# A layer's recurrence: the first two chunks' block products, exponentials and square roots put together

## Chip, cores and metric

The kernel runs on one core of a Trainium2 chip. The time is that of the device for one execution, in microseconds (us); of the kernel before it is 901.03, the median of three runs.

## What is computed

One layer over 512 positions of width 1024, in float32. After an RMS norm, one projection feeds three token mixers and their gates; then come the branches' projections, an output projection and a gated feed-forward part. The change is in the second mixer, a gated linear recurrence:

```python
r = jax.nn.sigmoid(jnp.einsum('bshi,hij->bshj', xb, w_rg).reshape(B, S, LRU_WIDTH) + b_rg)
i = jax.nn.sigmoid(jnp.einsum('bshi,hij->bshj', xb, w_ig).reshape(B, S, LRU_WIDTH) + b_ig)
log_a = (-LRU_C * r.astype(jnp.float32)) * jax.nn.softplus(-lru_lambda.astype(jnp.float32))
a = jnp.exp(log_a)
mult = jnp.sqrt(-jnp.expm1(2.0 * log_a))
b = mult * (i * xc).astype(jnp.float32)
# h[t] = a[t] * h[t-1] + b[t]
```

`xc` is a convolution of width 4 of the projection, and `w_rg` and `w_ig` are block-diagonal, 16 blocks of 64 x 64.

## The kernel before

Everything lies with channels on the 128 partitions and the 512 positions along the free axis. Each float32 product is made of three products of rounded parts: an operand is split on ACT into a high part (`whi`, L110) and on DVE into the rest (`wlo`, L111), and `mm3` (L278 to L280) multiplies high by high, high by low and low by high.

The stage of the change computes, on PE and in this order, four chunks of the recurrence's projection (`ps_lru`, two blocks of 128 channels each, so 256 of 1024) and four chunks of a branch's gate logits (`ps_gate_1`), as lru 0, 1, 2, gate 0, lru 3, gate 1, 2, 3. A chunk is 48 matmuls in two halves of 24, each half with a weight tile of its own; the halves are numbered, so that `whi14` and `whi15` are those of gate 0, 16 and 17 those of lru 3, 18 and 19 those of gate 1. Three weight tiles (`wp`, `bufs=3`) go round: the split of number n waits until PE has used number n - 3. Then the q, k and v projections (`ps_q`) begin, with weight halves 24, 25, 26 and so on.

The work of the recurrence on the other engines is cut into steps and laid in between. `lru_chunk(c)` (L596 on) emits the 48 matmuls of chunk c and gives back four functions:

- `conv` (L609): the convolution on DVE, out of PSUM;
- `split` (L615, L616): `xch` and `xcl`, the two parts of `xc`, on DVE;
- `both`: `gates(0)` and `gates(1)`, the products with the blocks (`lg`, L626: two PSUM tiles, each of three pairs of instructions of 64 rows, and the two of a pair run side by side), and on ACT eight sigmoids of 64 x 512 (`lr` L630, `li` L631);
- `tanh` (L635 on DVE, L638 on ACT).

Further steps are `lru_exp` (exponentials L655, square roots L661 on ACT), `lru_decay` (L666, L668 on DVE), `lru_input` (L674, L675 on DVE), `lru_scan` (L681 on DVE) and `lru_store` (L687 on ACT, L688 on DVE, two DMAs on POOL's queue). ACT holds one set of function tables at a time; sigmoid and tanh are in one set here, the exponential and the square root in two others, and where the next function is in another set an `ACT_TABLE_LOAD` stands ahead of it.

A list `bg` holds the steps. `step(...)` appends one entry, which may hold several functions, and `tick()` runs entries; an lru or gate chunk ticks four times, once behind each 12 matmuls. What a chunk's ticks run are thus the entries that were listed before it. `gate1(c)` (L717) emits a gate chunk and, behind it, `gate_store` (L570: two sigmoids of the PSUM tile into `gt1c`, and a store). The code's order is only the start: each engine's rows are arranged by a scheduler with priorities (weight splits get 60 and 200, `conv`, `split` and the first product of the convolution 300). Each engine then runs its rows strictly in the order in which they stand.

PSUM in this stage is a pool `pb` of four buffers of two banks each, named here by their first bank: 0, 2, 4, 6. A chunk takes one buffer; so does each of the two `lg` tiles of a chunk. A tile can only be written when the last reader of the one before it in its buffer is done. The recurrence's SBUF tiles come from 13 buffers of 4 KB a partition in the same manner.

Of the kernel before, what the change touches and what calls it, by code (L numbers as in the profile page):

```python
# [66 lines left out]
def layer_kernel(ctx: ExitStack, tc: tile.TileContext, x, xt, vecs, w_in, w_qkv7, w_gate7, w_pool, w_rg, w_ig,  # L67
# [340 lines left out]
    with ExitStack() as first:  # L408
# [308 lines left out]
        def gate1(c):  # L717
            gate_store(1, c, chan_chunk(("gate", 1, c), hn, 1, pb), True)
# [3 lines left out]
        def step(*fs):  # L722
            bg.append(lambda: [f() for f in fs])

        def of(f, c):
            return lambda: f(c)

        c0, s0, g0, t0 = lru_chunk(0)
        step(c0), step(s0), step(), step()
        c1, s1, g1, t1 = lru_chunk(1)  # L730
        step(c1), step(s1), step(g0), step(t0)
        c2, s2, g2, t2 = lru_chunk(2)
        step(of(lru_exp, (0,))), step(c2), step(s2), step(g1)
        gate1(0)
        step(of(lru_decay, 0), t1), step(of(lru_exp, (1,))), step(g2), step(of(lru_input, 0))
        c3, s3, g3, t3 = lru_chunk(3)
        step(c3), step(s3), step(of(lru_decay, 1), of(lru_scan, 0)), step(t2, of(lru_input, 1))
        gate1(1)
        step(of(lru_scan, 1)), step(g3, of(lru_store, 0)), step(t3, of(lru_store, 1)), step(of(lru_exp, (2, 3)))
        gate1(2)  # L740
        for f, c in ((lru_decay, 2), (lru_decay, 3), (lru_input, 2)):
            step(of(f, c))
# [927 lines left out]
```

## Time and profile before

| | |
|---|---|
| median of three runs (lowest, highest) | 901.03 us (900.64, 901.3) |
| the profiled execution | 900.73 us |
| its span, from the first instruction to the last | 899.0 us |
| PE busy | 893.4 us, 99% |
| DVE busy | 732.3 us, 81% |
| ACT busy | 523.2 us, 58% |
| POOL busy | 86.3 us, 10% |
| granted PE clock | full in every slice |

The page counts a matmul as busy from its start to its modelled end, 0.39 us, while they start 0.227 us apart; small waits of PE are hidden in that, and are read from the starts. In rows of the timeline the first number is the start from the beginning of the span, the second the duration; what stands in brackets is the idle time ahead and what ended it. A few per cent of the matmul records can be missing.

### The profile page before, as it was taken

Reading aid. Unit: us, or ns where it says so; the run is one execution under the profiler, and the core shown is the slowest. Engines: PE = TensorE matmul, PEld = TensorE weight load, DVE = VectorE, ACT = ScalarE, POOL = GpSimd, SP = SyncE. Lnnn points to the kernel's source line nnn. Section 1 sums busy time; section 2 is a strip of 40 time slices with the busy share of each in tenths; the row PEclk is TensorE's granted clock in tenths of the full one; section 3 lists DMA queues with packets and bytes.
Section 4 is the critical chain, followed back from the end, with each engine's and each line's share of the span. In section 5 each row is a group of like instructions: output and inputs, shape, how many; then the busy total and the mean of one; then the engine's idle time right before and its main releaser. Section 6 shows DMA issues by size and latency. Waiting matters only on the chain.

```text
span 899.0 us, 14052 instructions
## 1 busy us (share of the span) xinstructions
PE 893.4 (99%) x5491; PEld 794.2 (88%) x5491; DVE 732.3 (81%) x922; ACT 523.2 (58%) x722; POOL 86.3 (10%) x126
## 2 busy tenths in 40 slices
PE   9999999999999999999999999999999999999998
PEld 6888778788899888888888988889999999989998
DVE  7897897988786599967887696699888888799764
ACT  7554989556856556555664544454555555664532
POOL 1110002232332101000001100000000000101200
PEclk9999999999999999999999999999999999999999
DMA  9585347789682785734736865245543333866842
GB/s 337 147 303 156 115 127 215 234 286 242 181 260 71 233 235 190 220 118 141 223 91 152 184 177 170 94 131 152 141 117 95 111 102 125 225 167 122 180 99 94
DMA packets 116579, 151.98 MB, mean 169 GB/s; under 512 B 8096, under 2 KB 90016, under 8 KB 116512
## 3 DMA queue, kind: packets, MB, share of 16 engines
q1 hardware_dynamic: 104416, 107.30, 37.7%
q0 software_dynamic: 11952, 43.52, 20.6%
q8 instruction: 43, 0.70, 0.3%
q10 hardware_dynamic: 144, 0.26, 0.1%
q14 instruction: 24, 0.20, 0.1%
HBM read 130.61 MB, written 18.87 MB: 166 GB/s over the span
## 4 chain that ended last, share of the span: by engine, by line
PE 95%; DVE 2%; ACT 2%; issue 1%; DMA 0%; SPq 0%; DVEq 0%; ACTq 0%
PE ps_y L287 11%; PE ps_x L287 8%; PE ps_q L798 7%; PE ps_dy L287 5%; PE ps_dx L287 4%; PE ps_br L278 3%; PE ps_br L279 3%; PE ps_br L280 3%; PE ps_gate L701 2%; PE ps_bY L1238 2%; PE ps_gy L287 2%; PE ps_gate L280 2%; PE ps_bX L1238 2%; PE ps_gx L287 2%; PE ps_gate L279 2%; PE ps_gate L278 2%
## 5 line engine op out<-in xcount | busy, mean ns | idle before, releaser
L110 ACT ACTIVATE whi<-raw 128x1024 fp32r<-128x1024 f32 x73 | 77.2, 1058 | 85.3 <-PE ps_out L279 17.0
L111 DVE TENSOR_TENSOR wlo<-raw,whi 128x1024 fp32r<-128x1024 f32 x73 | 89.1, 1220 | 32.9 <-ACT whi L110 32.9
L111 DVE TENSOR_TENSOR wlo<-qw,whi 128x1024 fp32r<-128x1024 f32 x48 | 58.6, 1222 | 20.8 <-ACT whi L110 20.5
L110 ACT ACTIVATE whi<-qw 128x1024 fp32r<-128x1024 f32 x48 | 50.8, 1057 | 33.1 <-PE ps_q L798 18.6
L1403 ACT ACTIVATE wh_S<-w_S 128x1024 fp32r<-128x1024 f32 x36 | 38.2, 1064 | 35.5 <-PE ps_y L287 22.4
L1404 DVE TENSOR_TENSOR wl_S<-w_S,wh_S 128x1024 fp32r<-128x1024 f32 x36 | 43.8, 1220 | 6.2 <-ACT wh_S L1403 6.2
L1403 ACT ACTIVATE wh<-w 128x1024 fp32r<-128x1024 f32 x27 | 28.8, 1066 | 30.3 <-issue 11.9
L1494 POOL DMA_DIRECT2D dw<-in_w_down_dram x16 | 13.5, 846 | 325.9 <-DVE wl L1404 248.2
L1404 DVE TENSOR_TENSOR wl<-w,wh 128x1024 fp32r<-128x1024 f32 x27 | 32.9, 1220 | 10.0 <-ACT wh L1403 10.0
L1403 ACT ACTIVATE whdS<-dw 128x1024 fp32r<-128x1024 f32 x16 | 17.0, 1064 | 24.4 <-PE ps_dy L287 13.2
L1404 DVE TENSOR_TENSOR wldS<-dw,whdS 128x1024 fp32r<-128x1024 f32 x16 | 19.6, 1224 | 12.9 <-ACT whdS L1403 12.9
L1054 DVE TENSOR_TENSOR_SCAN E<-K,ahead 128x512 f32<-128x512 f32 (+3 forms) x32 | 25.3, 812 | 4.4 <-ACT K L1050 4.4
L278 PE MATMUL ps_br<-yHH,whi 128*128 128x512 f32 x64 | 25.3, 395 | 0.0
L278 PE MATMUL ps_lru<-HH,whi 128*128 128x512 f32 x64 | 25.2, 394 | 0.0
L278 PE MATMUL ps_br<-yph,whi 128*128 128x512 f32 x64 | 25.2, 394 | 0.0
L278 PE MATMUL ps_pool<-HH,whi 128*128 128x512 f32 x64 | 25.2, 393 | 0.0
L279 PE MATMUL ps_br<-ypl,whi 128*128 128x512 f32 x64 | 25.0, 391 | 0.0
L280 PE MATMUL ps_gate<-HH,wlo 128*128 128x512 f32 x64 | 25.0, 391 | 0.0
L278 PE MATMUL ps_gate<-HH,whi 128*128 128x512 f32 x64 | 25.0, 391 | 0.0
L280 PE MATMUL ps_br<-yph,wlo 128*128 128x512 f32 x64 | 25.0, 391 | 0.0
L279 PE MATMUL ps_br<-yHL,whi 128*128 128x512 f32 x64 | 25.0, 390 | 0.0
L279 PE MATMUL ps_pool<-HL,whi 128*128 128x512 f32 x64 | 25.0, 390 | 0.0
(717 smaller groups left out, 3426.3 us busy)
## 6 DMA issues: line engine op xcount, KB each, us to landing
raw<-in_w_in_dram SPq DMA_DIRECT2D x31, 512.0 KB, 5.2
qw<-in_w_qkv_dram SPq DMA_DIRECT2D x24, 512.0 KB, 6.8
w<-in_w_ffn_gate_dram SPq DMA_DIRECT2D x36, 256.0 KB, 4.1
w<-in_w_ffn_up_dram SPq DMA_DIRECT2D x36, 256.0 KB, 4.6
raw<-in_w_branch_dram SPq DMA_DIRECT2D x16, 512.0 KB, 4.4
dw<-in_w_down_dram POOLq DMA_DIRECT2D x16, 512.0 KB, 6.3
qw<-in_w_qkv_dram POOLq DMA_DIRECT2D x12, 512.0 KB, 7.6
qd<-r POOLq DMA_DIRECT2D x12, 512.0 KB, 7.2
```

Source lines behind the costliest of these rows:

```text
L110: act(hi, raw, AF.Copy)
L111: dve.tensor_tensor(lo, raw, hi.bitcast(F32), ALU.subtract)
L278: nc.tensor.matmul(ps, lh, rh, start=start, stop=False, skip_group_check=skip)
L279: nc.tensor.matmul(ps, lh, rl, start=False, stop=False, skip_group_check=skip)
L280: nc.tensor.matmul(ps, ll, rh, start=False, stop=stop, skip_group_check=skip)
L287: nc.tensor.matmul(o, a_[a][:, w, k, :], b_[b][:, k, :], start=first and n == k == 0, stop=last and n == 2 and k == 3, skip_group_check=True)
L701: nc.tensor.matmul(pss[n // 2][n % 2], w[:, k % 2, n * P:(n + 1) * P], hu[k][x_], start=k == 0 and w is wh and x_ == 0, stop=k == KT - 1 a ...
L798: nc.tensor.matmul(ps[:, a, :], b_[:, k, ts_], a_[:, kk, :], start=first and n == k == 0, stop=n == 2 and k == 3, skip_group_check=True)
L1054: dve.tensor_tensor_scan(E[:, c0:c0 + n][:, ::-1], K[:, c0 + 1:c0 + n + 1][:, ::-1], ahead[:, S - n:][:, ::-1], 0.0, ALU.mult, ALU.add)
L1238: nc.tensor.matmul(o, ah[x_][:, w, k, :], b[k][y_], start=first_ and n == k == 0, stop=n == 2 and k == 3, skip_group_check=True)
L1403: act(h, src, AF.Copy)
L1404: dve.tensor_tensor(l, src, h.bitcast(F32), ALU.subtract)
```

## The change

Only the list of steps is written in another order. The block products of chunks 0 and 1 (`g0`, `g1`) become one entry, run in gate 0's ticks and not in those of lru 2 and gate 0; their tanh (`t0`, `t1`) and then their exponentials and square roots (`lru_exp` of (0, 1), in place of one call for each) follow, and the steps behind them move by what that takes.

```diff
         c1, s1, g1, t1 = lru_chunk(1)
-        step(c1), step(s1), step(g0), step(t0)
+        step(c1), step(s1), step(), step()
         c2, s2, g2, t2 = lru_chunk(2)
-        step(of(lru_exp, (0,))), step(c2), step(s2), step(g1)
+        step(c2), step(g0, g1), step(s2, t0, t1), step(of(lru_exp, (0, 1)))
         gate1(0)
-        step(of(lru_decay, 0), t1), step(of(lru_exp, (1,))), step(g2), step(of(lru_input, 0))
+        step(of(lru_decay, 0)), step(of(lru_input, 0)), step(g2), step(of(lru_decay, 1), of(lru_scan, 0))
         c3, s3, g3, t3 = lru_chunk(3)
-        step(c3), step(s3), step(of(lru_decay, 1), of(lru_scan, 0)), step(t2, of(lru_input, 1))
+        step(c3), step(s3, of(lru_input, 1)), step(t2), step(of(lru_scan, 1))
         gate1(1)
-        step(of(lru_scan, 1)), step(g3, of(lru_store, 0)), step(t3, of(lru_store, 1)), step(of(lru_exp, (2, 3)))
+        step(of(lru_store, 0)), step(g3, of(lru_store, 1)), step(t3), step(of(lru_exp, (2, 3)))
         gate1(2)
```

**PE, around gate 0.** In the rows, `lg10` is chunk 1's first tile of block products and `lg11` its second; HH0 and HL0 are the two parts of the input's first half, HH1 and HL1 those of the second. Before, at the end of gate 0 (chunk 0's products are already done, in the middle of lru 2):

```order
L280 MATMUL ps_gate_1_0_809<-HH1_105,wlo15_753 128x512
L626 MATMUL lg10_886<-xch1_744,lwh_525 128x512 x2
L626 MATMUL lg10_886<-xcl1_745,lwh_525 128x512 x2
L626 MATMUL lg10_886<-xch1_744,lwl_526 128x512 x2
L626 MATMUL lg11_897<-xch1_744,lwh_525 128x512 x2
L626 MATMUL lg11_897<-xcl1_745,lwh_525 128x512 x2
L626 MATMUL lg11_897<-xch1_744,lwl_526 128x512 x2
L278 MATMUL ps_lru_3_912<-HH0_104,whi16_812 128x512
```

In the change, in the middle of gate 0 (behind the three rows of `lg00`, chunk 0's first tile, of which the last is shown):

```order
L626 MATMUL lg00_820<-xch0_668,lwl_526 128x512 x2
L626 MATMUL lg01_831<-xch0_668,lwh_525 128x512 x2
L626 MATMUL lg01_831<-xcl0_669,lwh_525 128x512 x2
L626 MATMUL lg01_831<-xch0_668,lwl_526 128x512 x2
L626 MATMUL lg10_842<-xch1_744,lwh_525 128x512 x2
L626 MATMUL lg10_842<-xcl1_745,lwh_525 128x512 x2
L626 MATMUL lg10_842<-xch1_744,lwl_526 128x512 x2
L626 MATMUL lg11_853<-xch1_744,lwh_525 128x512 x2
L626 MATMUL lg11_853<-xcl1_745,lwh_525 128x512 x2
L626 MATMUL lg11_853<-xch1_744,lwl_526 128x512 x2
L278 MATMUL ps_gate_1_0_783<-HH1_105,whi15_752 128x512
```

Four tiles of products now stand together, while gate 0's own tile is half done.

**ACT, behind the sigmoids of chunk 1.** `gt10` is gate 0's output, the last reader of its PSUM tile; `lt`, `lr` and `ls` are the tanh, the exponential and the square root, with the chunk's number. Before:

```order
L631 ACTIVATE li1_749<-lg11_897,bigx_206 64x512
L570 ACTIVATE gt10_908<-ps_gate_1_0_809,vt_69 128x512 x2
L110 ACTIVATE whi19_955<-raw19_953 128x1024
L638 ACTIVATE lt1_933<-lr1_748,cpos_112 128x512 x2
L655 ACT_TABLE_LOAD
L655 ACTIVATE lr1_748<-lr1_748,cneg_113 128x512 x2
L661 ACT_TABLE_LOAD
L661 ACTIVATE ls1_951<-lt1_933 128x1024
L630 ACT_TABLE_LOAD
L630 ACTIVATE lr2_872<-lg20_971,vt_69 64x512
```

In the change:

```order
L638 ACTIVATE lt1_892<-lr1_748,cpos_112 128x512 x2
L655 ACT_TABLE_LOAD
L655 ACTIVATE lr0_672<-lr0_672,cneg_113 128x512 x2
L110 ACTIVATE whi19_957<-raw19_955 128x1024
L655 ACTIVATE lr1_748<-lr1_748,cneg_113 128x512 x2
L661 ACT_TABLE_LOAD
L661 ACTIVATE ls0_912<-lt0_888 128x1024
L661 ACTIVATE ls1_914<-lt1_892 128x1024
L570 ACT_TABLE_LOAD
L570 ACTIVATE gt10_916<-ps_gate_1_0_783,vt_69 128x512 x2
L110 ACTIVATE whi20_1017<-raw20_1015 128x1024
L630 ACTIVATE lr2_886<-lg20_973,vt_69 64x512
```

`gt10`, which stood ahead of chunk 1's tanh, now stands behind the tanh, exponentials and square roots of both chunks. Ahead of the piece shown stand sixteen sigmoids (L630, L631) and chunk 0's tanh, with the split `whi18` between; the table loads from the first exponential to chunk 3's are six where they were nine.

**DVE, during gates 1 and 2.** `xch3` and `xcl3` are chunk 3's split, `wlo22` is gate 3's first weight. Before:

```order
L615 CAST xch3_1047<-xc3_1007 128x1024
L111 TENSOR_TENSOR wlo21_1056<-raw21_1053,whi21_1055 128x1024
L616 TENSOR_TENSOR xcl3_1048<-xc3_1007,xch3_1047 128x1024
L111 TENSOR_TENSOR wlo22_1101<-raw22_1098,whi22_1100 128x1024
L635 TENSOR_TENSOR li2_873<-li2_873,xc2_806 128x1024
L675 TENSOR_TENSOR ls1_951<-ls1_951,li1_749 128x1024
L681 SCALAR_TENSOR_TENSOR li1_749<-lt1_933,ls1_951 128x512 x2
```

In the change:

```order
L616 TENSOR_TENSOR xcl3_1052<-xc3_1011,xch3_1051 128x1024
L668 TENSOR_SCALAR lt1_892<-lt1_892 128x1024
L111 TENSOR_TENSOR wlo22_1103<-raw22_1100,whi22_1102 128x1024
L681 SCALAR_TENSOR_TENSOR li0_673<-lt0_888,ls0_912 128x512 x2
L674 SCALAR_TENSOR_TENSOR ls1_914<-lr1_748,ls1_914 128x1024
L635 TENSOR_TENSOR li2_887<-li2_887,xc2_780 128x1024
L675 TENSOR_TENSOR ls1_914<-ls1_914,li1_749 128x1024
L111 TENSOR_TENSOR wlo23_1165<-raw23_1162,whi23_1164 128x1024
L681 SCALAR_TENSOR_TENSOR li1_749<-lt1_892,ls1_914 128x512 x2
```

Chunk 0's scans (the rows of L681 that write `li0`) now stand behind `wlo22`. The tanh of chunk 2 on ACT takes the SBUF buffer of `lt0`, so it waits for these scans; before, it took another one. On ACT the split `whi22` stands ahead of that tanh, and behind it `gt11`, `whi23`, the copy `yh0` (L687) and chunk 3's sigmoids; before, `yh0` stood behind chunk 3's sigmoids.

**PSUM.** The rows name tiles, not buffers. Which buffer a tile gets goes by which is free first, and the built programs give:

| tile | before: buffer, tile ahead of it in there | change: buffer, tile ahead of it in there |
|---|---|---|
| ps_lru_0, ps_lru_1, ps_lru_2 | 6, 4, 2 | 6, 4, 2 |
| lg00, lg01 | 0; 6, lru_0 | 6, lru_0; 4, lru_1 |
| ps_gate_1_0 | 4, lru_1 | 0 |
| lg10, lg11 | 0, lg00; 6, lg01 | 2, lru_2; 6, lg00 |
| ps_lru_3 | 2, lru_2 | 4, lg01 |
| ps_gate_1_1 | 4, gate_1_0 | 0, gate_1_0 |
| ps_gx1, ps_gy1 (the last tiles of this pool) | 0; 4 | 2; 0 |
| ps_pool_1_0 (the first of the next stage) | bank 0, behind gx1 | bank 0, behind gy1 |

gx1 and gy1 are the last products of the third branch's gates; DVE reads them at L847, and the pool mixer's projection `ps_pool` follows on PE.

## The prediction

> **What bounds the kernel now.** I read the busy times first, then the view of waits for TensorE (PE) alone, then stretches of the part that the change touches, with the busy time of PE, PEld, DVE, ACT and POOL in that order.
>
> ```profile
> PE 893.4 (99%) x5491; PEld 794.2 (88%) x5491; DVE 732.3 (81%) x922; ACT 523.2 (58%) x722; POOL 86.3 (10%) x126
> ...
> PE warm_ps L422 <- DVE warm L301: 1.5, 1, 1.5
> PE ps_gate L701 <- ACT hu L437: 0.5, 1, 0.5
> PE ps_q L798 <- DVE wlo L111: 0.4, 1, 0.4
> ...
> 126.00:151.00 25.00, 25.00 (x115) 19.88 (x114) 17.37 (x16) 24.29 (x30) 4.68 (x7) 1.00 0.66 212
> ```
>
> PE is the bound: 893.4 of 899.0 us, and the waits listed sum to 2.4. After 168 us it waits for nothing that the view lists, so whatever PE loses or gains here reaches the end of the run whole. The last row says who is next: from 126 to 151 us ACT works 24.29 of 25 us. A step that puts more in front of ACT there will be waited for.
>
> A matmul starts every 0.227 us. Looking for longer steps between starts finds what the waits view is too coarse for (columns: start, duration).
>
> ```profile
> 120.96 0.39 PE L279 MATMUL ps_gate<-HL,whi 128*128 128x512 f32 x1
> 121.32 0.50 PE L280 MATMUL ps_gate<-HH,wlo 128*128 128x512 f32 x1
> 121.66 0.39 PE L278 MATMUL ps_gate<-HH,whi 128*128 128x512 f32 x1
> ...
> 150.02 0.39 PE L798 MATMUL ps_q<-whi,HH 128*128 128x512 f32 x1
> 150.40 0.50 PE L798 MATMUL ps_q<-wlo,HH 128*128 128x512 f32 x1
> 150.74 0.39 PE L798 MATMUL ps_q<-whi,HL 128*128 128x512 f32 x1
> ...
> 166.64 0.39 PE L798 MATMUL ps_q<-whi,hT3h 128*128 128x512 f32 x1
> 167.39 0.50 PE L798 MATMUL ps_q<-wlo,hT3h 128*128 128x512 f32 x1 [0.36 <-DVE wlo L111]
> 167.72 0.39 PE L798 MATMUL ps_q<-whi,hT3l 128*128 128x512 f32 x1
> ```
>
> Two steps of each should take 0.45 and take 0.70, 0.72 and 1.08: losses of 0.25, 0.27 and 0.63, 1.15 together. Of each, 0.11 is the step after the wait (0.34 in place of 0.227), so I add 0.1 to every wait below. All three wait for a weight split on DVE behind work of the recurrence.
>
> **The change part by part.** First the block products themselves:
>
> ```profile
> 71.78 0.39 PE L278 MATMUL ps_lru<-HH,whi 128*128 128x512 f32 x1
> ...
> 79.71 0.39 PE L280 MATMUL ps_lru<-HH,wlo 128*128 128x512 f32 x1
> 80.03 0.50 PE L626 MATMUL lg<-xch,lwh 64*128 64x512 f32 x2
> 80.36 0.40 PE L626 MATMUL lg<-xcl,lwh 64*128 64x512 f32 x2
> ...
> 81.29 0.40 PE L626 MATMUL lg<-xch,lwl 64*128 64x512 f32 x2
> 81.62 0.50 PE L278 MATMUL ps_lru<-HH,whi 128*128 128x512 f32 x1
> 81.95 0.40 PE L279 MATMUL ps_lru<-HL,whi 128*128 128x512 f32 x1
> 82.19 0.39 PE L280 MATMUL ps_lru<-HH,wlo 128*128 128x512 f32 x1
> ```
>
> From 79.71 to 82.19 are nine steps: 2.48 us where 2.04 would be the pace. Entering and leaving the 64-row form costs 0.44. With chunks 0 and 1 in one block it is paid three times, not four: **saved 0.44**.
>
> The block moves behind the 48 matmuls of lru_2 (first at 71.78) and 24 of gate_1_0: 71.78 + 72 x 0.227 + 0.09 = 88.2. Its slots run at 0.33, then 0.2325, so lg11, the tenth, would start at 90.4. But buffer 6, in which it is computed, holds lg00 until ACT has read it in four sigmoids.
>
> ```profile
> 81.04 0.69 ACT L630 ACTIVATE lr<-lg,vt 64x512 f32<-64x512 f32 x1 [2.79 <-PE lg L626]
> ...
> 85.24 0.68 ACT L630 ACTIVATE lr<-lg,vt 64x512 f32<-64x512 f32 x1
> ...
> 87.74 1.34 ACT L638 ACTIVATE lt<-lr,cpos 128x512 f32<-128x512 f32 x2
> 89.10 1.28 ACT L655 ACT_TABLE_LOAD   x1
> 90.39 1.34 ACT L655 ACTIVATE lr<-lr,cneg 128x512 f32<-128x512 f32 x2
> 91.64 1.05 ACT L110 ACTIVATE whi<-raw 128x1024 fp32r<-128x1024 f32 x1
> ...
> 103.32 1.27 ACT L570 ACTIVATE gt<-ps_gate,vt 128x512 f32<-128x512 f32 x2
> ...
> 143.49 2.01 ACT L661 ACTIVATE ls<-lt 128x1024 f32<-128x1024 f32 x2
> ```
>
> The first sigmoid came 1.01 after the first product (81.04 against 80.03), and six steps later it is 85.24: 0.70 each. In the change: first sigmoid 89.2 (the split whi17 ahead of it ends at about the same time), four done at 92.0, wait 1.65. **Term A: 1.65 + 0.1 = +1.75.** lg10 takes lru_2's buffer, which DVE must have left.
>
> ```profile
> 88.19 1.52 DVE L602 TENSOR_SCALAR xc<-ps_lru,vt 128x512 f32<-128x512 f32 x2
> 89.63 4.02 DVE L609 SCALAR_TENSOR_TENSOR xc<-ps_lru,vt,xc 128x511 f32<-128x511 f32 x6
> ```
>
> That takes 5.5 us and can start at lru_2's end, 82.9, so it is over by 88.4; lg10 starts at 89.7. No cost, with 1.3 us of cover.
>
> Next gate_1_1. It takes buffer 0, which gate_1_0 holds until ACT has written gt10, and gt10 now stands behind everything of the recurrence. On ACT from 89.2: sixteen sigmoids 11.2 (100.4), four tanh 2.68 and a weight split 1.05 (104.1), a table load 1.29 (105.4), four exponentials 2.68 and a split 1.05 (109.2), a load 1.29, two square roots 2.01, a load 1.29 (113.8), gt10 1.27: 115.0. On PE: lg11 from 92.05, 0.8 for its three slots, 0.2 for leaving, 72 matmuls 16.3, chunk 2's products 1.36 + 0.44: it arrives at 111.2. **Term B: 3.8 + 0.1 = +3.9.** A and B hang together: a shorter A lengthens B by as much, since ACT's count is fixed by the first sigmoid. Durations without overlap make it the upper end; with 0.09 saved between equal instructions the sum A + B falls from 5.65 to about 5.0.
>
> The page of the Trainium skill on ScalarE ("ScalarE: Activation LUTs", section "What ACT_TABLE_LOAD costs") adds a drain of about 1.38 us to each load of about 1.28. By it the three loads ahead of gt10 would take 4.1 more, term B would be 8.0 and the time 912.4, an estimate from that page. The trace disagrees: the tanh pair ends at 89.08, the load runs from 89.10 and the exponential starts at 90.39, with no drain between, so this case gets no chance.
>
> Then the third product stage. Call the start of gate_1_2 P. ACT's split whi22 waits for its buffer until P; behind it DVE's wlo22 and now chunk 0's two scans, and ACT's tanh of chunk 2 takes over the buffer that lt0 leaves after those scans.
>
> ```profile
> 127.58 2.34 DVE L681 TENSOR_TENSOR_SCAN li<-lt,ls 128x512 f32<-128x512 f32 x2
> ...
> 144.59 1.23 DVE L666 SCALAR_TENSOR_TENSOR lt<-lr,lt 128x1024 f32<-128x1024 f32 x1 [1.15 <-ACT ls L661]
> ...
> 149.13 1.22 DVE L111 TENSOR_TENSOR wlo<-qw,whi 128x1024 fp32r<-128x1024 f32 x1
> ```
>
> So tanh starts at P + 1.05 + 1.22 + 2.34 = P + 4.6. From there ACT is never free: tanh, gt11, a split, yh0, eight sigmoids (5.6), yh1, a split, tanh, a load, four exponentials with a split, a load, one square root: 21.1 by the durations, some 20.5 with overlaps. DVE then needs 5.8 from the square root to the end of wlo26 (144.56 to 150.35). That is P + 30.9; PE needs wlo26 after 121 matmuls and chunk 3's products, P + 29.3. **Term C: 1.6 + 0.1 = +1.7**, between 0.8 and 2.2 by how much overlaps. It replaces the old wait at 150 us, and the old ones at 121 and 167 fall away, since PE now comes later than what they waited for: **saved 1.15**.
>
> Last, far behind, the pool's buffers have changed places: the first pool product takes buffer 0, which held gx1 before and holds gy1 now.
>
> ```profile
> 295.84 1.22 DVE L847 TENSOR_TENSOR gx<-gx,ps_gx 128x1024 f32<-128x1024 f32 x1 [0.52 <-PE ps_gx L287]
> ...
> 298.36 0.40 PE L278 MATMUL ps_pool<-HH,whi 128*128 128x512 f32 x1
> ...
> 298.56 1.22 DVE L847 TENSOR_TENSOR gy<-gy,ps_gy 128x1024 f32<-128x1024 f32 x1 [0.37 <-PE ps_gy L287]
> ```
>
> gx was read by 297.06, before 298.36. gy is read only by 299.78, and its read follows PE's own last product. **Term D: 299.8 - 298.36 + 0.1 = +1.5.**
>
> Hidden: three table loads fewer (3.9 us of ACT) are inside the counts. The stores of gd and yd on POOL (10% busy) and two weight loads that SP issues earlier cost nothing, as PE's waits name no DMA; a load late by more than a split's lead of about 2 us would be seen.
>
> Sum: 1.75 + 3.9 + 1.7 + 1.5 - 0.44 - 1.15 = **+7.3 us**. The profiled execution took 900.73 (span 899.0), 0.3 below the median of 901.03: 908.0 for such an execution, **908.3** for the median.
>
> **The rivals.**
>
> *Later waits don't come.* If ACT overlaps more than I count, and DVE reads gy1 while PE is elsewhere, C and D go: 908.3 - 3.2 = 905.1. For it: C is a small difference of two long sums. Against D's going: its two ends are both rows.
>
> *The clock drops in B's wait.* PE stands still for 3.8 us, longer than anywhere here.
>
> ```profile
> 1.46 3.41 PE L422 MATMUL warm_ps<-warm 128*128 128x512 bf16 x9 [1.46 <-DVE warm L301]
> ```
>
> The nine matmuls after the idle start took 3.41, 0.38 each; at 0.227 that is 1.4 lost. Once more of it gives 909.7. The Trainium skill ("TensorE: Matmul & The Clock Gate", section "HAM oscillation — how this bites in real kernels") says that idle gaps above about 3.4 us throttle the engine again. No run here shows such a gap; the granted clock is full in every slice.
>
> *ACT's relief decides, and it gets faster.* ACT does 3.9 us less. If gt10 were written before PE needs buffer 0, the new waits would be gone with the old: 901.03 - 0.44 - 1.15 = 899.4. It decides at 111.2: gt10 would have to come 3.8 earlier, ahead of the exponentials. ACT's rows put it behind them, so this needs an order that the program does not have. A wait for gt10 under 1.6 with C and D absent would come out even.
>
> **How the numbers follow.** The forecast (906 to 909.4) has 0.70, the clock 0.12, the later waits' absence 0.11, faster 0.03, even 0.01; 0.03 lies above. The range reaches from the second case to the clock's with A + B and C at their ends: 905.0 to 910.7. A measurement here tells 0.2% (1.8 us) from no change: faster 0.03, same 0.01, slower 0.96.
>
> **What would show it.** PE's waits should list lg (L626) for the sigmoids of L631, about 1.6; ps_gate (L278) for ACT gt (L570), about 3.8; ps_q for DVE wlo, about 1.6; ps_pool for DVE gy (L847), about 1.4; and two table loads each at L655 and L661 and none at L630, where there were three, three and two. Starts some 0.38 apart behind the long wait would be the clock. A wait of PE for a DMA, or none for gt10, would make the prediction wrong.

## The result, and the profile after

The changed kernel takes 910.33 us (median of four executions, 909.43 to 910.82) against 900.84 beside it: 1.0102 times as long, 95% interval 1.009 to 1.0114. 908.3 was predicted, with 905.0 to 910.7 as the range. The direction and all four waits of the forecast are there. On top of the forecast's terms, PE's record has a fall of its clock, which stood among the rivals.

The busy times of the changed kernel, and its view of waits for PE:

```profile
PE 895.4 (99%) x5491; PEld 795.7 (88%) x5491; DVE 732.4 (81%) x922; ACT 519.1 (57%) x719; POOL 86.5 (10%) x126
```

```profile
PE ps_gate L278 <- ACT gt L570: 3.4, 1, 3.4
PE lg L626 <- ACT li L631: 1.5, 1, 1.5
PE warm_ps L422 <- DVE warm L301: 1.5, 1, 1.5
PE ps_q L798 <- DVE wlo L111: 1.4, 1, 1.4
PE ps_pool L278 <- DVE gy L847: 1.3, 1, 1.3
```

Four waits are new. ACT has three instructions fewer, the table loads, and 4.1 us less to do, and the kernel is slower. The starts on PE at the four places (start, duration; in brackets the wait):

```profile
90.25 0.40 PE L626 MATMUL lg<-xch,lwl 64*128 64x512 f32 x2
92.14 0.50 PE L626 MATMUL lg<-xch,lwh 64*128 64x512 f32 x2 [1.49 <-ACT li L631]
...
114.84 0.75 PE L278 MATMUL ps_gate<-HH,whi 128*128 128x512 f32 x1 [3.37 <-ACT gt L570]
115.38 0.63 PE L279 MATMUL ps_gate<-HL,whi 128*128 128x512 f32 x1
115.81 0.63 PE L280 MATMUL ps_gate<-HH,wlo 128*128 128x512 f32 x1
...
118.36 0.40 PE L280 MATMUL ps_gate<-HH,wlo 128*128 128x512 f32 x1
118.59 0.40 PE L278 MATMUL ps_gate<-HH,whi 128*128 128x512 f32 x1
...
156.46 0.39 PE L798 MATMUL ps_q<-whi,HH 128*128 128x512 f32 x1
158.25 0.50 PE L798 MATMUL ps_q<-wlo,HH 128*128 128x512 f32 x1 [1.40 <-DVE wlo L111]
...
305.43 0.28 PE L287 MATMUL ps_gy<-hT4h,wlo 128*128 128x256 f32 x1
307.01 0.50 PE L278 MATMUL ps_pool<-HH,whi 128*128 128x512 f32 x1 [1.31 <-DVE gy L847]
```

From 115.38 on, behind the longest wait, the starts are 0.43 us apart and not 0.23. The stretches of the same place (the last three numbers are the granted clock, the DMA share and GB/s):

```profile
115.00:115.50 0.50, 0.50 (x2) 0.41 (x3) 0.50 (x2) 0.50 (x1) 0.42 (x1) 0.50 0.00 0
115.50:118.50 3.00, 3.00 (x9) 2.36 (x8) 3.00 (x4) 2.92 (x6) 0.34 (x1) 0.53 0.46 175
118.50:119.00 0.50, 0.50 (x4) 0.41 (x3) 0.50 (x2) 0.50 (x1) 0.00 (x0) 1.00 0.00 0
```

PE runs at half clock, and added up over quarter-microsecond stretches that lasts 3.41 us. The nine steps from 114.84 to 118.59 take 3.75 us in place of 2.04: 1.7 lost. This is the execution of 909.43, with a mean clock of 0.998; in the three others the mean is 0.996, which is 6.83 us of half clock, and they take 910.18 to 910.82, 0.8 to 1.4 us more.

### The profile page after: what moved, and what is told of

Same layout as the page of the kernel before. It is cut to its first block, busy times and chain, and to the rows that moved or that the text cites. A ratio compares the mean times of both kernels' runs of the same rounds, so it can differ in the third digit from the quotient of the medians.

```text
span 907.6 us, 14052 instructions
## 1 busy us (share of the span) xinstructions
PE 895.4 (99%) x5491; PEld 795.7 (88%) x5491; DVE 732.4 (81%) x922; ACT 519.1 (57%) x719; POOL 86.5 (10%) x126
## 4 chain that ended last, share of the span: by engine, by line
PE 93%; ACT 5%; DVE 1%; issue 1%; DVEq 0%; ACTq 0%
PE ps_y L287 11%; PE ps_q L798 8%; PE ps_x L287 8%; PE ps_dy L287 5%; PE ps_dx L287 4%; PE ps_br L278 3%; PE ps_br L279 3%; PE ps_br L280 3%; PE ps_gate L701 2%; PE ps_bY L1238 2%; PE ps_gy L287 2%; PE ps_bX L1238 2%; PE ps_gx L287 2%; PE ps_pool L278 2%; PE ps_pool L280 2%; PE ps_pool L279 2%
## 5 line engine op out<-in xcount | busy, mean ns | idle before, releaser
L279 PE MATMUL ps_gate<-HL,whi 128*128 128x512 f32 x64 | 25.6, 400 | 0.0
```

Of the source, the lines that this page charges most:

```text
L279: nc.tensor.matmul(ps, lh, rl, start=False, stop=False, skip_group_check=skip)
```

## The experiments

Gains and losses are read against the kernel before, run beside each on the same chip (900.8 to 901.4 us): the changed kernel is 9.5 us above it. Half clock of 3.41 us takes 1.7 us of PE's time, and it comes in some executions of a kernel and not in others, so differences under 1 us between kernels are not read.

**The two halves of the change, each alone, on the kernel before.** First the exponentials and roots in one step, the block products left apart.

```diff
-        step(of(lru_exp, (0,))), step(c2), step(s2), step(g1)
+        step(), step(c2), step(s2), step(g1)
-        step(of(lru_decay, 0), t1), step(of(lru_exp, (1,))), step(g2), step(of(lru_input, 0))
+        step(t1), step(of(lru_exp, (0, 1))), step(g2, of(lru_decay, 0)), step(of(lru_input, 0))
```

> The kernel before with one part of the change: the exponentials and square roots of chunks 0 and 1 in one step (behind gate_1_0's store and chunk 1's tangents), the block products left apart. Three table loads fewer, gt10 not delayed, PSUM buffers as before. Theory (the loss comes from what waits for ACT at PSUM buffers, and from the late scan of chunk 0): no wait at gate_1_1 and none at the first pool product, a wait at the q product's chunk 12 between 0.3 and 2 us because chunk 0's scan comes later; time 900.9 to 903.0. Rival (putting the exponentials together is what costs, through the recurrence's chain): 904 or more, with waits for weight splits of 3 us and more between 145 and 180 us.

Measured: 904.18 us, 3.1 above the kernel before; ratio 1.0035 (1.0022 to 1.0048). PE's waits:

```profile
PE ps_q L798 <- DVE wlo L111: 0.9, 1, 0.9
PE ps_q L798 <- ACT whi L110: 0.9, 1, 0.9
```

Neither theory named 904.18 well: the mechanism is the first one's (no wait at gate_1_1, none at the pool), the time the rival's. In the profiled execution (904.57 us) restarts and half clock for 3.41 us from 152.4 us on come on top of the waits' 1.9 us. Half clock is not what the loss hangs on, though: two of the five executions ran at full clock throughout and took 903.9 and 904.31.

Then the block products in one step, the exponentials left apart.

```diff
-        step(c1), step(s1), step(g0), step(t0)
+        step(c1), step(s1), step(), step()
-        step(of(lru_exp, (0,))), step(c2), step(s2), step(g1)
+        step(c2), step(g0, g1), step(s2, t0), step(of(lru_exp, (0,)))
```

> The kernel before with the other part of the change: the block products of chunks 0 and 1 in one step, and chunk 0's tangent and exponential behind them; the exponentials of chunk 1 stay in a step of their own behind gate_1_0's store. Theory: lg11 waits 1.5 us as in the changed kernel (1.77 in all), one entry and exit of the 64-row form is saved (0.44), gt10 stands on ACT behind one chunk's exponentials and ends near 110.5, so gate_1_1 waits for at most 0.3; the PSUM buffers turn as in the changed kernel, so the first pool product waits 1.3 us (1.5 in all); three older stalls of 1.15 go or change. Sum 900.9 + 1.8 - 0.4 + 1.5 - 1.2 = 902.6, plus what the weight splits between 145 and 180 us are late: 0 to 3.5, 902.6 to 906. Rival (the step that merges the block products makes the 3.5-us wait as well): a wait of 2 us or more at gate_1_1 and 907 or above.

Measured: 906.03 us, 5.0 above; ratio 1.0055 (1.0042 to 1.0068). The clock stayed up.

```profile
PE lg L626 <- ACT li L631: 1.5, 1, 1.5
...
PE ps_pool L278 <- DVE gy L847: 1.3, 1, 1.3
PE ps_gate L278 <- ACT li L631: 1.1, 1, 1.1
PE lg L626 <- DVE xcl L616: 0.9, 1, 0.9
```

The time is at the upper end of the theory's (906), and the rival's wait at gate_1_1 did not come. The last two rows are waits that the changed kernel does not have: at gate_1_2 (123.8 us) for sigmoids and at chunk 3's products (131.2 us) for their split. The text before the run allowed for late weight splits, not for these.

So the terms have owners. The waits at lg11 (A) and at the pool (D) come with the block products. The late weight splits in the q product (C) come with the exponentials. The long wait at gate_1_1 (B) is in neither: it needs both, sixteen sigmoids late and both chunks' exponentials ahead of gt10. The halves cost 3.1 and 5.0 alone and 9.5 together.

**Term A.** The block products in two steps, all else as changed.

```diff
-        step(c2), step(g0, g1), step(s2, t0, t1), step(of(lru_exp, (0, 1)))
+        step(c2, g0), step(g1), step(s2, t0, t1), step(of(lru_exp, (0, 1)))
```

> The changed kernel with the block products of chunks 0 and 1 in two steps again (chunk 0's one step earlier), all else as changed. Theory (lg11 waits because its PSUM buffer holds lg00 until four sigmoids have read it, and ACT's chain to gt10 starts at the first of them): the 1.5-us wait at lg11 goes (1.77 in all), one more entry and exit of the 64-row form comes back (0.44), the first sigmoid runs 2.7 us earlier and with it gt10, so gate_1_1 starts near 112.1 after a wait of 2.4 us in place of 3.5. Time 910.3 - 1.8 + 0.4 - 1.1 = 907.8 if the clock still falls, 905.2 to 906.1 if 2.4 us is too short for that. Rival (the lg11 wait only hides the later one, so that undoing it moves 1.7 us from lg11 to gate_1_1): gate_1_1 still starts at 114.84 with a wait above 4.5 us, and the time stays at 910.3 + 0.4 or a little above.

Measured: 907.92 us, ratio 1.0077 (1.0064 to 1.009). The wait at lg11 is gone, and gate_1_1 starts at 113.45 after a wait of 3.10 us and a fall of the clock: the first theory's 907.8. The rival's 114.84 did not come. Gate_1_1 started only 1.4 us earlier, not 2.7, so the wait there stayed longer than expected; the waits for weight splits in the q product stayed as well (1.2 us).

**Term D.** The unused tile ahead of the second token gate left out, so that gx1 and gy1 change buffers.

```diff
-            if cc:
-                dve.memset(pb.tile([P, 2, S], F32, tag="mm", name="skip_g")[:, 0, 0:1], 0.0)
```

> The changed kernel without the unused PSUM tile and its one-element memset ahead of the second token gate: gx1 and gy1 change buffers, so that the first pool product takes over the buffer of gx1 (read last at 304.2) and the second that of gy1. Nothing else moves. Theory (step D: that product waits for gy1's addition only because of the buffer): the 1.3-us wait at the first pool product goes, 1.5 us in all, to 908.8 within 0.4. Rival (DVE's addition is waited for anyway, by the second pool tile 2.7 us later or by the weights behind it on DVE): a wait of 0.5 us or more appears within 6 us behind it and the time stays at 909.8 or above.

Measured: 908.75 us, ratio 1.0085 (1.0071 to 1.0099): 1.6 less than the changed kernel, as expected. No wait is listed at the pool.

**Term B.** The exponentials queued behind gt10 (chunk 0's decay and input share an entry, so that the number of entries stays).

```diff
-        step(c2), step(g0, g1), step(s2, t0, t1), step(of(lru_exp, (0, 1)))
+        step(c2), step(g0, g1), step(s2, t0, t1), step()
-        step(of(lru_decay, 0)), step(of(lru_input, 0)), step(g2), step(of(lru_decay, 1), of(lru_scan, 0))
+        step(of(lru_exp, (0, 1))), step(of(lru_decay, 0), of(lru_input, 0)), step(g2), step(of(lru_decay, 1), of(lru_scan, 0))
```

> The changed kernel with one step moved: the exponentials and square roots of chunks 0 and 1 are queued behind gate_1_0's store instead of ahead of it, so gt10's two sigmoids stand right behind chunk 1's tangents on ACT (about 104.1 us) and no longer behind 9.4 us of loads, exponentials and roots. Theory (ACT's order makes the 3.5-us wait, and the wait makes the clock fall): PE's wait for ACT gt L570 falls from 3.4 us to under 0.3, the granted clock stays at 1.0 from 111 to 120 us, and the time falls by 3.5 for the wait and 1.7 to 2.6 for the clock, to 904.2 to 905.1. Rival (ACT simply has too much work between 89 and 115 us): the wait comes back at the next PSUM buffer that ACT has to free (gate_1_2 or lg30) with 2 us or more, and the time stays at 907 or above. The waits at lg11 (1.5), at the q product (about 1.4) and at the first pool product (1.3) stay.

Measured: 908.34 us, ratio 1.0081 (1.0068 to 1.0095). The wait at gate_1_1 is gone, and in four of five executions half clock too, and only 2.0 of the expected 5.2 to 6.1 us came. The rest went here:

```profile
PE ps_q L798 <- DVE wlo L111: 2.5, 2, 1.5
...
PE ps_q2S L798 <- DVE wlo L111: 1.0, 1, 1.0
PE ps_q L798 <- ACT whi L110: 0.6, 1, 0.6
```

4.1 us of waits for weight splits in the q products, where the changed kernel has 1.4. The theory of B was right about B and wrong about its worth: a second limit, the late splits, let only 2.0 us of it through.

**The clock.** PE's idle time filled: chunk 2's block products, which stand right ahead of the wait, computed twice (three times in the second kernel).

```diff
-                for n, (w, x_) in enumerate((("h", "h"), ("h", "l"), ("l", "h"))):
+                for n, (w, x_) in list(enumerate((("h", "h"), ("h", "l"), ("l", "h")))) * (2 if c == 2 else 1):
```

> The changed kernel with chunk 2's twelve 64-row block products computed twice (the second pass starts the sums anew and gives the same values): about 1.4 us more of PE work right ahead of the 3.5-us wait, none on ACT. PE's idle time ahead of gate_1_1 falls to about 2.1 us, while the time at which ACT's gt10 ends and gate_1_1 starts (114.84) stays. Theory (the clock falls because PE stands idle long enough): if 2.1 us is short enough, no slice between 115 and 119 us has a clock below 0.95 and the time falls by 1.7 to 2.6, to 907.7 to 908.6, although PE has 1.4 us more to do. Rival (the fall has another cause, or costs nothing beyond the wait): the starts behind the wait stay 0.43 us apart and the time stays at 910.3 within 0.4. Third outcome, 2.1 us is still too long: as the rival here, and the next kernel tells.

> As the kernel before it, with chunk 2's block products computed three times: about 2.8 us more of PE work ahead of the wait, PE idle for about 0.7 us, gate_1_1 still starting at 114.84. Theory (length of PE's idle time sets the clock): clock 1.0 throughout, time 907.7 to 908.6, and equal within 0.4 to the kernel with two passes if 2.1 us was short enough there. Rival (the clock's fall has nothing to do with the idle time): the starts behind the wait stay 0.43 us apart, time 910.3 within 0.4.

Measured with two passes: gate_1_1 starts at 114.73 as before, after a wait of 2.01 us, and the next starts are 0.34 and 0.24 apart: no fall, by the mean clock in three of four executions. Yet the time is 909.76 us, ratio 1.0098 (1.0084 to 1.0111): waits for weight splits between 154 and 175 us grew from 1.4 to 2.7 us and took the gain back. One of them, 0.8 us at 175 us, is the old stall of 167 us, which the changed kernel does not show. With three passes: 911.64 us, ratio 1.0114 (1.01 to 1.0127). The wait at gate_1_1 is 0.7 us, without a fall; but a new wait of 1.84 us for a weight split, at 128.7, is followed by a fall:

```profile
128.72 0.50 PE L280 MATMUL ps_gate<-HH,wlo 128*128 128x512 f32 x1 [1.84 <-DVE wlo L111]
129.06 0.40 PE L278 MATMUL ps_gate<-HH,whi 128*128 128x512 f32 x1
129.30 0.49 PE L279 MATMUL ps_gate<-HL,whi 128*128 128x512 f32 x1
129.59 0.63 PE L280 MATMUL ps_gate<-HH,wlo 128*128 128x512 f32 x1
130.01 0.63 PE L278 MATMUL ps_gate<-HH,whi 128*128 128x512 f32 x1
```

A wait of 2.01 without a fall and one of 1.84 with it: length alone does not decide. So it was measured by itself, behind the kernel before.

```diff
...
+    for m in range(21):
+        ps = fp.tile([P, 2, S], F32, tag="mm", name=f"zps{m}")
+        for _ in range((60, 47, 75)[m // 7]):
+            nc.tensor.matmul(ps[:, 0, :], onesr, zr, start=True, stop=True)
+        zr = zp.tile([P, S], F32R, tag="z", name=f"zr{m}")
+        act(zr, ps[:, 0, :], AF.Copy, scale=1.0 / P)
+        for _ in range((0, 1, 2, 3, 4, 5, 7)[m % 7]):
+            act(zr, zr.bitcast(F32), AF.Copy)
```

> The kernel before, its output unchanged, with a test stretch behind it: 21 blocks of back-to-back 128x512 matmuls (60 in each of the first seven, 47 in the next seven, 75 in the last), and between two blocks a chain of 1, 2, 3, 4, 5, 6 or 8 copies on ACT that the next block has to wait for, so that PE stands idle for about 1, 1.7, 2.4, 3, 3.7, 4.4 and 5.8 us, each length three times. Theory 1 (length alone): there is one length, above 1.9 us and at most 3.4, from which on every wait is followed by half clock and below which none is. Theory 2 (the share of work within stretches of a fixed time that run on by themselves, about 3.3 us each, so that it counts how a wait lies to them): waits of 2 to 3.7 us are followed by half clock in some of the three cases and not in others, those of 1 us in none, those of 5.8 us in all, and half clock lasts about 3.3 us or a multiple of it. Rival (nothing to do with waits): falls at other places than behind waits, or none.

Blocks of this stretch on PE (start, duration of the block, matmuls, and the wait ahead of it):

```profile
928.64 13.89 PE L1636 MATMUL zps<-zr,onesr 128*128 128x512 f32 x60 [1.35 <-ACT zr L1640]
944.54 15.48 PE L1636 MATMUL zps<-zr,onesr 128*128 128x512 f32 x60 [2.01 <-ACT zr L1640]
...
1048.71 10.95 PE L1636 MATMUL zps<-zr,onesr 128*128 128x512 f32 x47 [1.35 <-ACT zr L1640]
1061.67 10.95 PE L1636 MATMUL zps<-zr,onesr 128*128 128x512 f32 x47 [2.01 <-ACT zr L1640]
...
1183.65 18.92 PE L1636 MATMUL zps<-zr,onesr 128*128 128x512 f32 x75 [2.01 <-ACT zr L1640]
```

Behind 1.35 us a block of 60 takes 13.89 us and one of 47 takes 10.95. Behind 2.01 us, the block of 60 takes 1.6 longer and that of 47 does not; the block of 75 (17.29 behind 1.35 us) takes 1.6 longer again. All waits (behind the last no block stands), with half clock added up over stretches of a quarter microsecond:

| wait, us | 0.69 | 1.35 | 2.01 | 2.67 | 3.33 | 3.99 | 5.31 |
|---|---|---|---|---|---|---|---|
| followed by half clock | 0 of 3 | 0 of 3 | 2 of 3 | 3 of 3 | 3 of 3 | 3 of 3 | 2 of 2 |
| of these for 6.83 us, else 3.41 | | | 0 | 1 | 0 | 2 | 1 |

Theory 1 fails at 2.01 us, and the fall lasts 3.41 us or twice that, never anything between, as the second theory has it. That waits of 2.67 and 3.33 us differ among themselves, as it also has it, did not show here. In the kernels of this study one of 3.38 us (the late stores, below) was not followed by a fall.

The traces decide it. All changes of the granted clock within one, the rise at the start included, lie whole multiples of 3.4133 us apart: in the changed kernel the rise is at 5.69 us, and the fall at 114.92 and the next rise at 118.33 come 32.00 and 33.00 of them later. So each trace can be cut into such windows, and the idle time of PE, as the view of waits counts it, added up in each. Of the windows at full clock, up to PE's last work, all twenty with 2.00 us of idle time or more were followed by half clock and none with 1.75 or less; between them 1.84 and 1.88 were, and 1.89 was not. A window at half clock was followed by a second one in all five cases with 0.62 us of idle time or more, and in none with 0.52 or less. The windows around gate_1_1's start (length, PE busy, and third from the end the granted clock) in the changed kernel, in the one with the late stores, and in the one with gx1's buffer exchanged (term D):

```profile
111.50:114.92 3.42, 0.08 (x1) 1.00 0.08 29
114.92:118.33 3.41, 3.41 (x8) 0.50 0.40 154
...
110.02:113.44 3.42, 1.79 (x8) 1.00 0.51 153
113.44:116.85 3.41, 1.66 (x7) 1.00 0.03 13
...
110.62:114.04 3.42, 0.95 (x5) 1.00 0.40 135
114.04:117.45 3.41, 2.57 (x6) 0.50 0.30 114
117.45:120.86 3.41, 3.41 (x9) 0.50 0.11 40
```

| wait, us | where | idle time in the windows it lies in, us | half clock, us |
|---|---|---|---|
| 3.37 | changed kernel | 0.04, 3.33 | 3.41 |
| 3.31 | gx1's buffer exchanged | 2.47, 0.84 | 6.83 |
| 3.38 | late stores | 1.62, 1.75 | none |
| 2.01 | products twice | 0.89, 1.12 | none |
| 2.01 | test stretch, blocks of 60 and 75 | 2.01 | 3.41 |
| 2.01 | test stretch, block of 47 | 1.60, 0.41 | none |
| 1.84 | products three times | 1.84 | 3.41 |
| 0.94 and 0.94 | exponentials alone | 1.88 in one | 3.41 |

What half clock costs a whole kernel is another question. Between executions of one kernel, a portion of 3.41 us more went with 0.7 to 1.9 us more time in the changed kernel, with the products twice and three times and with the late stores. In four other kernels the executions at full clock were no faster: 908.84 against 907.68 to 908.21 with the products apart (term A), 903.9 and 904.31 against 904.05 to 904.57 with the exponentials alone, 908.44 against 907.88 to 908.26 with those of chunks 2 and 3 left out, and 906.56 against 905.69 to 906.21 with chunk 0's scan first (the last two are told below). A likely reason is that the next late split takes up what PE gains; none of these at full clock was profiled, so this is not shown.

**Term C.** The copies of the stores moved off the path to wlo26.

```diff
-        step(of(lru_store, 0)), step(g3, of(lru_store, 1)), step(t3), step(of(lru_exp, (2, 3)))
+        step(), step(g3), step(t3), step(of(lru_exp, (2, 3)))
-        for f, c in ((lru_decay, 2), (lru_decay, 3), (lru_input, 2)):
+        for f, c in ((lru_decay, 2), (lru_decay, 3), (lru_input, 2), (lru_store, 0), (lru_store, 1)):
```

> The changed kernel with the stores of chunks 0 and 1 (a copy of 1.05 us on ACT, a subtraction of 1.2 us on DVE and two DMAs each) moved behind the exponentials of chunks 2 and 3, into gate_1_3's steps. Theory (step C: the copies yh0 and yh1 stand on ACT at 135.41 and 141.97, ahead of everything that leads to wlo26, so wlo26 comes 2.1 us too late): the wait at the q product's chunk 12 falls from 1.4 us to under 0.3 and the time by 1.3 to 1.7, to 908.6 to 909.0. Rival (after the first runs: DVE is busy nearly without a gap from 152 to 178 us, so its backlog and not one position decides): the wait goes at that place and comes back by the same amount between 160 and 180 us, and the time stays between 909.7 and 910.5.

Measured: 913.19 us, ratio 1.0133 (1.0119 to 1.0146), worse than either theory.

```profile
PE ps_gate L278 <- ACT gt L570: 3.4, 1, 3.4
PE ps_q L798 <- ACT r L811: 2.8, 1, 2.8
...
PE ps_q L798 <- DVE wlo L111: 0.4, 1, 0.4
```

The wait of C shrank to 0.4 as the theory says, and the copies, now at 156.49 and 159.32 on ACT, made the copy out of PSUM late instead: 2.8 us, with half clock behind it (this is the execution of 911.85). Next, in the kernel with gt10 first, the exponentials of chunks 2 and 3 were left out.

```diff
-                for j in range(2):
+                for j in range(2 if c < 2 else 0):
                     r = lru[c]["r"][:, j, :]
...
             for c in cs:
+                if c >= 2:
+                    lru[c]["s"] = lru[c]["r"]
+                    continue
                 lru[c]["s"] = b4([2, S], f"ls{c}")
```

> The kernel with gt10 ahead of the exponentials (908.3 us, waits for weight splits of 4.1 us in all between 151 and 179 us), and with the exponentials and square roots of chunks 2 and 3 left out, so that these chunks' results are not those of the recurrence: some 8.5 us less on ACT between 140 and 156 us (4 exponentials of 0.67, 2 roots of 1.0, 3 table loads of 1.28), nothing less on DVE. Theory (ACT's queue of chunks 2 and 3 makes the weight splits late, and took the gain of that kernel back): the waits at 152 to 159 us go, 3.7 us with their restarts, and the time falls to 903.6 to 904.8. Rival (DVE's backlog makes the splits late): the waits stay within 1 us in all, 907.3 or more.

Measured: 908.16 us, ratio 1.0077 (1.0065 to 1.0089), no gain on 908.34. The waits in the q products fell from 4.1 to 2.3 us, so they are neither gone, as the theory has it, nor where they were, as the rival has it; and half clock came in addition. Freeing ACT of 8.5 us removes less than half of the waits, and the longest one left (1.9 us) is for DVE. Then three edits together: block products apart, gt10 first, gx1's buffer.

> The changed kernel with three edits of earlier runs together: block products of chunks 0 and 1 in two steps, gt10 ahead of the exponentials, and the first pool product's buffer from gx1. What is left of the change is the exponentials and roots of chunks 0 and 1 in one step. If each gain adds up: 910.3 - 2.4 - 2.0 - 1.6 = 904.3. If the weight splits between 145 and 180 us stay the bound whatever PE gains ahead of them: the first two gains share one limit, 906 to 907, with waits for weight splits of over 4 us there. If the two waits and the clock were all of it: 903 or below. It is the same set of steps as the kernel before with only the exponentials together (904.2 us), in another order.

Measured: 907.28 us, ratio 1.0069 (1.0057 to 1.0082): just above the shared limit of 906 to 907 and 3.0 us above the sum of the gains, with 4.4 us of waits for splits and half clock behind them. Last, chunk 0's scan ahead of chunk 3's convolution on DVE, on top of these three:

```diff
+        def soon(*fs):
+            with tc.high_priority(EARLY):
+                for f in fs:
+                    f(0)
...
-        step(of(lru_exp, (0, 1))), step(of(lru_decay, 0), of(lru_input, 0)), step(g2), step(of(lru_decay, 1), of(lru_scan, 0))
+        step(of(lru_exp, (0, 1))), step(lambda: soon(lru_decay, lru_input, lru_scan)), step(g2), step(of(lru_decay, 1))
```

> The kernel with three edits together (907.3 us) and one more: chunk 0's decay, input and scan run on DVE at the priority of the convolution, so that the scan stands ahead of chunk 3's convolution (about 116.5 us) instead of at 125 to 129 us. In that kernel ACT stands idle for 7.61 us until 129.38, when the scan has released the buffer that chunk 2's tangent writes, and all of ACT's work up to 160 us follows from there; PE then waits for weight splits for 0.75, 2.22 and 1.40 us (5.4 us in all with the restarts) and has half clock from 155 to 159 us (1.7 us). Theory (the merged step makes chunk 0's scan late, the scan holds chunk 2's tangent, and that is what makes the weight splits late): ACT's tangent starts near 122, chunk 3's sigmoids 5 us earlier, the waits between 145 and 180 us fall under 1.2 us in all, the clock stays up: 900.2 to 902.5. Rival (the sum of ACT's and DVE's work up to 160 us makes them late, wherever the scan stands): waits of 3 us and more stay there, 904.5 or more.

Measured: 905.72 us, ratio 1.005 (1.0036 to 1.0064). PE's waits, and ACT's rows around chunk 2's tangent:

```profile
PE ps_gate L280 <- DVE wlo L111: 2.2, 1, 2.2
...
PE ps_q L803 <- DVE wlo L111: 1.3, 3, 0.8
```

```profile
120.88 0.71 ACT L638 ACTIVATE lt<-lr,cpos 128x512 f32<-128x512 f32 x1
...
130.73 1.06 ACT L687 ACTIVATE yh<-li 128x1024 fp32r<-128x1024 f32 x1 [6.45 <-DVE ls L674]
```

The tangent starts at 120.9 and not at 129.4, and the q product's waits fall from 4.4 to 1.3 us, close to the theory's 1.2 and far from the rival's 3. But the scan has pushed a weight split back, PE waits 2.2 us for it from 121.6 us on, half clock follows, and ACT then stands idle for 6.45 us behind DVE. So the time is the rival's, by another way than it says. The stretches 95 to 110 and 125 to 140 us (third group: DVE's busy time) of the kernel before, of the changed one, and of this last one:

```profile
95.00:110.00 15.00, 15.00 (x76) 11.37 (x75) 12.38 (x12) 14.52 (x20) 0.76 (x1) 1.00 0.42 132
125.00:140.00 15.00, 15.00 (x72) 11.91 (x71) 10.73 (x10) 13.34 (x18) 2.43 (x5) 1.00 0.85 295
```

```profile
95.00:110.00 15.00, 15.00 (x72) 11.89 (x71) 6.67 (x6) 14.81 (x20) 0.00 (x0) 1.00 0.11 37
125.00:140.00 15.00, 15.00 (x72) 11.90 (x71) 12.88 (x12) 8.90 (x13) 1.32 (x2) 1.00 0.54 170
```

```profile
95.00:110.00 15.00, 15.00 (x72) 11.90 (x71) 5.55 (x5) 14.83 (x21) 0.76 (x1) 1.00 0.33 106
125.00:140.00 15.00, 15.00 (x66) 11.78 (x65) 14.22 (x14) 9.13 (x13) 1.87 (x4) 0.91 0.88 284
```

From 95 to 110 us DVE was busy for 12.38 us of 15 before, with chunk 0's recurrence among it. With the exponentials together it is starved there (6.67 and 5.55), and does that work from 111 us on, where the convolution of chunk 3 and weight splits are due: from 111 to 126 us it is busy for 14.71 us of 15 in the changed kernel (14.21 before) and for all 15.00 in the last one. It is not full for long. From 126 to 152 us of the changed kernel DVE is busy for 16.60 of 26 us and ACT for 20.80 (third and fourth group), each waiting for the other in turn:

```profile
126.00:152.00 26.00, 26.00 (x121) 20.99 (x120) 16.60 (x15) 20.80 (x27) 2.94 (x5) 1.00 0.59 203
```

So what is late is the chain that goes back and forth between the two engines, set back where DVE is full, and not a lasting overload of either. That DVE's share is the cause is read from these stretches; no run took work off DVE. No order tried here gets that time back, and none of the variants beats the kernel before.

## Why the prediction was right, and where it was short

- **Entry and exit of the 64-row form, -0.44, and the old stalls, -1.15:** as predicted. No step at the three old places stands out any more, but for the one that became C. The third of them is away only while PE comes late there: with the products apart, twice or three times, or the scan first, it is back with a wait of 0.8 us at 173 to 177 us.
- **A, +1.75:** 90.25 to 92.14 is 1.89 where the pace is 0.23, and the restart 0.11 more: 1.8. With the products apart the wait was gone, and 2.4 of the 2.5 us expected of that edit came.
- **B, +3.9:** 111.08 to 114.84 is 3.76, so 3.5 over the pace. The count of ACT's rows came 0.2 us too late (gt10 was over at 114.8, not 115.0). A and B were to sum to between 5.0 and 5.65, and sum to 5.3.
- **C, +1.7:** 156.46 to 158.25, 1.6 over the pace and 0.1 for the restart. Size and chain are those of the forecast: gate_1_2 starts at 127.4, chunk 2's tangent 4.6 us later, ACT has no idle time of note from there to the square root, and wlo26 is done at 158.2, 30.7 us after gate_1_2's start where 30.9 was counted. What the sum does not have is how close the next limits stand: with ACT's copies moved, ACT's exponentials left out or the scan moved, waits for other things came in place of this one.
- **D, +1.5:** 1.6, and 1.6 came back when the buffers were exchanged.
- **The clock, a rival with 0.12 and 1.4 us:** this is the step that failed. Half clock came in every execution, by the mean clock 3.41 us of it in one and 6.83 us in three, and took 1.7 us of PE's time in the profiled one. The terms over the pace are 1.8 + 3.5 + 1.7 + 1.7 + 1.6 - 0.4 - 1.2 = 8.7, against 8.6 between the spans (907.6 and 899.0); without the clock 7.0, against the predicted 7.3. The prediction gives no reason for a chance as low as 0.12, although the rule that it cites points to a fall for its wait of 3.8 us; its own profile had no wait of a running PE between 0.5 and 3.8 us from which to weigh it. Its price of 1.4 us is low because the nine matmuls of its row were not all at half clock: most start 0.43 us apart, the last two 0.28 and 0.22 behind the one before. By the windows, a wait of 3.37 us puts 2.00 us or more into one of them in some eight of ten positions (an estimate: it fails only where the part in the first window is between 1.37 and 2.00, 0.63 of 3.41). How much of the 2 us between 908.3 and 910.33 the clock is worth is open: with the products twice, gate_1_1 started at the same time without a fall, and the time was still 909.76, with 1.3 us more of waits for the splits behind. The Trainium skill ("TensorE: Matmul & The Clock Gate", section "What's actually happening") says that the clock is set by windows of 3413 ns that run on by themselves; the trace agrees, with falls of 3.41 and 6.83 us and nothing between. The rule that was cited beside the rival, gaps above about 3.4 us, is not what was measured: 1.84 and 2.01 us were enough.
- **What the sum could not say:** its terms fit as a record of where PE stood, and not as a list of what each is worth. B and the clock are 5.2 us of the record, and taking both away brought some 2, since the late splits behind them grew by 2.7. D, with nothing behind it, brought its whole 1.6, and A 2.4.
- **"ACT's relief decides", 0.03:** it did not happen by itself. Putting gt10 ahead of the exponentials made the order that this rival needed, and still gave 908.3, not 899.4, because A and D do not hang on gt10 and the late splits of C grew.

What stays open: why a window with 1.89 us of idle time was not followed by half clock where 1.84 and 1.88 were, where the three executions without a profile had their 6.83 us, and whether any order of DVE's work makes the joined exponentials free.

## What to carry to other kernels

Joining steps to save table loads or mode changes moves everything that follows from them later at once: look at which other engine lives on the first half of the joined result (here DVE, 5.7 us less busy in the 15 us from 95 us on, and full from 111 us on), and at which buffers their last readers hold. A wait of the bound engine is worth what it seems only if nothing stands close behind it, so find the next limit before counting the gain. Count 1.7 us of PE's time for half clock on top of a wait, or of several close together, that can put some 2 us of idle time into one window of 3.41 us, and remember that the kernel need not get it back when the wait goes.

## What was not expected of the hardware

Half clock came in portions of 3.41 us, one or two, on a grid of 3.413 us that runs through a whole trace. What counted was PE's idle time within one window of that grid, with the limit between 1.75 and 2.00 us: so a wait of 1.84 us and two waits of 0.94 in one window were followed by half clock, and a wait of 3.38 us that lay half in one window and half in the next was not. Behind a first portion, 0.62 us of idle time was enough for a second. At half clock, starts of 128x512 matmuls are 0.43 us apart in place of 0.227, so each portion takes 1.7 us of PE's time, but in four of the kernels the executions without it were no faster.
